# A gated delta rule on TensorE: products of 128 rows issued together, then products of 64 rows with the two heads by turns

## The chip, the cores and the metric

One core of a Trainium2 chip runs the whole program in one launch. The metric is the device time of that core in microseconds, the median of the runs shown.

## What is computed

The kernel is two layers of a block for a latent diffusion model, on 256 context tokens and 256 latent tokens of 1024 channels, in float32. Each layer has an input projection, four token mixers that read it (retention, HGRN2, the gated delta rule, RG-LRU), a merge with gates and an output projection, and then a feed-forward part with a convolution. The change touches the gated delta rule only. It has 4 heads with keys of 64 and values of 128 channels, scanned forward and backward, in chunks. One chunk of one head and direction, cut to what matters:

```python
def step(s, inp):
    qc, kc, vc, gc, bc = inp
    cum = jnp.cumsum(gc, axis=-1)
    rel = cum[..., :, None] - cum[..., None, :]
    a_mat = eye + (bc[..., :, None] * jnp.exp(jnp.where(strict, rel, -jnp.inf))
                   * jnp.einsum('bhtd,bhsd->bhts', kc, kc))
    rhs = bc[..., None] * (vc - jnp.exp(cum)[..., None] * jnp.einsum('bhtd,bhde->bhte', kc, s))
    u = lax.linalg.triangular_solve(a_mat, rhs, left_side=True, lower=True, unit_diagonal=True)
    qk = jnp.einsum('bhtd,bhsd->bhts', qc, kc) * jnp.exp(jnp.where(incl, rel, -jnp.inf))
    o = (jnp.exp(cum)[..., None] * jnp.einsum('bhtd,bhde->bhte', qc, s)
         + jnp.einsum('bhts,bhse->bhte', qk, u))
    last = cum[..., -1:]
    s_new = (jnp.exp(last)[..., None] * s
             + jnp.einsum('bhsd,bhse->bhde', kc * jnp.exp(last - cum)[..., None], u))
    return s_new, o
```

## The kernel before

The program writes its own order: jobs of large matrix products (projections, feed-forward; tiles gft, gtf, up) and threads of steps (the mixers, the layernorms) are emitted one step at a time by a loop that keeps an estimate of the engines' clocks and gives TensorE large products wherever a thread's step could not start yet (pump, L244). The order is fixed when the program is built; on the chip every engine works through its own queue in order and waits on semaphores. Nearly all instructions are issued through one helper, so the profile gives them line L82 and they are told apart by their tiles.

The delta rule (gdn, L1786) handles two heads at a time (group g, heads hh = 0 and 1), with a kernel chunk of 128 tokens. Per layer there are two groups, each with two segments (context, then latents) of two chunks. After the triangular systems are inverted (tile gd_T) the function recur (L2001) does one step of both directions d:

- U, a PSUM bank per head: for each direction a product of 128 rows, gd_T with the values (tile gd_v; L2012), and, when there is a state S already, a product of 64 rows, gd_W with gd_S (L2014). Head 0's operands of 64 rows lie in partitions 0 to 63, head 1's in 64 to 127. VectorE multiplies each head's bank by beta into gd_u (L2016).
- gd_dS (L2023), products with 64 columns per head, and from it the new state gd_S on VectorE (L2030) or, in the first step of a scan, ScalarE.

After both steps of a segment the readout (L2056 to L2067) forms gd_o, again a bank per head: for each chunk and direction a product of 128 rows (gd_P with gd_u) and, where that step had a state, one of 64 rows (gd_QT with gd_S). The function readout (L1272) then takes the squares (ro_sq, ScalarE, one instruction per head), the sums and the root on VectorE, scales (ro_n) and transposes on TensorE (ro_t). The last layer has no readout for the context.

The product call on float32 operands turns into two weight loads and two matmul records in the trace, so "x2" in a row is one product of the program. Products that only use 64 rows are marked 64\*128 there, those with 64 weight columns 128\*64, full ones 128\*128. A similar pair of heads exists elsewhere: gd_pk (L1884), the products of keys and queries, is issued head 0 first, then head 1, 64 rows each, one bank per head.

The loop that orders the two kinds of product in U is:

```python
for hh in range(2):
    U = self.pmt([128, 2, 128], "gd_U")
    for d in range(2):
        mm(U[:, d, :], R["TT"][...], v[...], start=True, stop=(S is None))
        if S is not None:
            mm(U[:, d, :], R["W"][p0:p0 + 64, ...], S[p0:p0 + 64, d, :], start=False, stop=True)
    V.tensor_tensor(u[:, :, hh, :], U, bb, op=ALU.mult)
```

PSUM banks for these come from one pool of four that all mixers share (pmt, L463).

Of the kernel before, what the change touches and what calls it, by code (L numbers as in the profile page):

```python
# [9 lines left out]
F32 = mybir.dt.float32  # L10
# [4 lines left out]
ALU = mybir.AluOpType  # L15
# [35 lines left out]
# by layer: the instances that follow one another in a pool  # L51
# [4 lines left out]
# the second layer's modulation blocks that fill the layernorms' waits  # L56
# [5 lines left out]
# from an engine's end to the start of the one that waits for it  # L62
# [9 lines left out]
class _Eng:  # L72
    """An engine of nc; every call also goes to the order's estimate of the engines' clocks."""
# [30 lines left out]
class _Pair:  # L104
    """the context's and the latents' jobs of one block"""
# [9 lines left out]
class Net:  # L115
# [17 lines left out]
    # ------------------------------------------- estimate of the engines' clocks  # L133
    def after(self, table, name, key):
        """when an engine sees that a tile is written (rdy) or read (rd)"""
        return max([t + LAT[p][key] for p, t in table.get(name, {}).items()] + [0.0])

    def names(self, x):
        """what the estimate knows an operand by: its tile, and the blocks of 256 for the activations"""
        nm = x.tensor.name  # L140
        if nm not in self.by_seg:
            return [nm]
        us = [x.offset // 256]
        for st, c in x.ap[1:-1]:
            us = [u + st // 256 * q for u in us for q in range(c)]
        st, n = x.ap[-1]
        m = (x.offset % 256 + st * (n - 1)) // 256 + 1
        return [f"{nm}.{u + q}" for u in us for q in range(m)]

    def account(self, key, name, a, k):  # L150
# [12 lines left out]
        if not dma:  # L163
            # engines take turns at a PSUM tile
# [72 lines left out]
    # ------------------------------------------------------------- the order  # L237
# [6 lines left out]
    def pump(self, until):  # L244
        """Emit the threads' steps and, where the tensor engine would wait for them, steps of matrix products."""
        while not until():
            # the step that can start first; products of matrices when none can start before the tensor engine is free
# [12 lines left out]
    def advance(self, t):  # L260
        outer, self.now_in = self.now_in, t
        try:
            t[1] = next(t[0])
            # a step's third word: the thread's bank is not used any more
# [6 lines left out]
    def finish(self, t, bank=False):  # L271
        """emit the rest of a thread, or its steps up to the last use of its bank"""
# [4 lines left out]
    def limit(self, key, n):  # L277
        """at most n threads of a kind are under way"""
# [5 lines left out]
    def when(self, t):  # L284
        """the engine of a thread's next step and the time when its operands are there (None: it waits for other steps)"""
# [8 lines left out]
    # -------------------------------------------------- matrix products' stream  # L294
# [20 lines left out]
    def feed(self):  # L315
        """keep loads three tiles ahead and splits two tiles ahead of the tile in use"""
# [15 lines left out]
    def splitter(self):  # L332
        """thread: the loaded tiles' two float32r parts, one tile ahead of the tile in use"""
# [15 lines left out]
    def gemm_start(self):  # L349
        """when the next step of the matrix products can start (None: it waits for a thread's step)"""  # L350
# [35 lines left out]
    def drain(self, jobs):  # L386
        """emit until these jobs are done"""
        self.pump(lambda: all(j.done for j in jobs))

    def store(self, pairs, then=None):  # L390
        """a thread that sends tiles to DRAM, [(to, from)], when they are there, so that the queue does not wait for them"""
# [25 lines left out]
    def evac(self, rec, ps, f, eng="ACT"):  # L417
        """a thread that empties a bank of products; its job is done when the thread is"""
# [13 lines left out]
    # --------------------------------------------------------------- helpers  # L432
# [5 lines left out]
    def xw(self, i, q, sg, d, n):  # L438
        """part q of blocks d .. d + n of a segment's modulated activations, to be written"""
        if i == 0:  # L440
            return self.X[0][q][:, d:d + n, sg * 256:(sg + 1) * 256]
        if sg not in self.X[i]:
            # a tile per segment: the context's place is used again
# [3 lines left out]
    def xr(self, q, k, t0, t1):  # L447
        """part q of block k of tokens t0 .. t1, as [(operand, first column)]"""
# [17 lines left out]
    def pgt(self, shape, name):  # L466
        """a bank of products and the list that its thread goes into"""
# [8 lines left out]
    def e2(self, shape, name, dt=F32):  # L476
        """a tile that lives within one step"""
        return self.tile(self.ep, shape, dt, "e2", name, 2)

    def ev(self, shape, name):  # L480
        """an evacuation thread's tile"""
# [23 lines left out]
    def load_consts(self):  # L505
        const, I, V, A, S = self.const, self.I, self.V, self.A, self.S
        # silu(c): columns (lat, ctx) and zeros up to a column tile of the tensor engine
# [25 lines left out]
    def derive(self):  # L533
        """small per-layer parameters"""
        const, V, A = self.const, self.V, self.A
        self.pd = []
        for i in range(DEPTH):
# [15 lines left out]
            hg = const.tile([128, 2, 8], F32, name=f"hgp{i}")   # B, -B with 1 - f = B - B tanh, B = (1 - lb) / 2  # L553
# [25 lines left out]
    def softplus(self, x, shape):  # L579
        """max(x, 0) + log1p(exp(-|x|)), log1p(e) = ln(w) + (e - (w - 1)) / w with w = 1 + e"""  # L580
# [17 lines left out]
    def rsq(self, v, n, scale=1.0, eps=EPS, post=None):  # L598
        """(v * scale + eps) ** -0.5 by a seed from the exponent bits and two Newton steps, the first one's constants fitted to the seed"""
# [18 lines left out]
    def tt(self, out, a, b, op, bias=POOL_BIAS):  # L618
        """tensor_tensor on the vector engine or on GpSimd, the one that would be done first"""
# [8 lines left out]
    def split(self, dstH, dstL, src32):  # L628
        """src32 into two float32r parts"""
# [3 lines left out]
    # ------------------------------------------------------- matrix products  # L633
    def gemm_ft(self, ps, HL, xH, xL, K, w=128, c0=0):
        """ps[f, t] = sum_k w[k, f] x[k, t], the weights stationary"""
# [3 lines left out]
        for k in range(K):  # L639
            h = H[:, k * w + c0:k * w + c0 + 128]  # L640
            for p, x in enumerate(xH(k) + xL(k)):
                # a start clears the written bits of the whole bank
# [13 lines left out]
    def in_ft(self, i, c0, tsl, evac, cond=None):  # L656
        """job: the [f, t] block of the input projection's columns c0 .. c0 + 128"""
# [11 lines left out]
    def gemm_tf(self, nks, tl, lH, lL, evac, eng="DVE"):  # L669
        """[t, 256 columns], the activations stationary, the weights moving; a bank holds two t tiles"""  # L670
# [4 lines left out]
        for n, nk in enumerate(nks):  # L675
            H, L = self.next_tile()
            for t in tl:
# [5 lines left out]
                for k in range(nk):  # L683
                    w = H[:, k * 256:(k + 1) * 256]
                    # a start clears the written bits of the whole bank
# [18 lines left out]
    # ------------------------------------------------------------- modulation  # L704
    def mod_jobs(self, i, nb, early=False):
        """512 columns nb of silu(c) @ w_mod[i]: shift and scale columns, or the gates' rows (kept in DRAM)"""
# [3 lines left out]
        def mk(kk):  # L710
            def run():
# [11 lines left out]
                # four rows' blocks side by side in the column tiles  # L723
# [8 lines left out]
            def evac(ps):  # L732
# [3 lines left out]
                if kind in (2, 5):  # L736
# [7 lines left out]
                    # half the gates: the products that they take carry the sigmoids' factor 2  # L744
# [20 lines left out]
    # -------------------------------------------------------------- layernorm  # L765
    def ln_rs(self, st):
        """(mean, 1 / std) of each token tile, from st [128, tile, groups, 6]"""
# [7 lines left out]
    def modulate(self, i, half, sg, xs):  # L775
        """layernorm0(x) * (1 + scale) + shift of segment sg, transposed to [d, t], in two float32r parts"""
# [48 lines left out]
    def seen(self, i, half, t0, t1):  # L825
        """whether the modulated activations of tokens t0 .. t1 are there"""
        return lambda: all((i, half, sg) in self.ok for sg in range(t0 // 256, (t1 + 255) // 256))

    def residual(self, i, half, xin, segs, when=lambda: True):
        """what the residual's sum needs beside the sub-layer's output"""  # L830
        self.grow = {}

        def load():
            yield when
            n = self.n_ran
            for sg in segs:
                if xin is not None:
                    self.r[sg] = self.tile(self.fa, [128, 2, 1024], F32, "f_r", "r", len(segs))
                    for j in range(2):
                        # a piece per job, between the weights  # L840
# [5 lines left out]
                # segment 0 is the context, column 1 of the modulation pair  # L846
# [37 lines left out]
    # ------------------------------------------------------------------ layers  # L884
    def body(self):
# [3 lines left out]
        # the first blocks' shift and scale go first  # L889
# [30 lines left out]
    def masks(self):  # L920
        """the masks, as bytes"""
# [8 lines left out]
    def mixers(self, prev):  # L930
# [24 lines left out]
        def closer():  # L955
            """the previous phase's end; then the space is there for the second group of mixers"""
# [50 lines left out]
    def merge_jobs(self, j, nm, pool):  # L1007
        """merged += sigmoid(gate) * (branch @ w_branch); the final branch also splits the sums"""
# [1214 lines left out]
```

## Time and profile before

| | before |
|---|---|
| median of 3 runs | 2274.57 us (2270.27 to 2276.27) |
| profiled execution, span from first to last instruction | 2267.0 us |
| median less that span (what lies around the span; no other time of the profiled execution is recorded) | 7.6 us |
| TensorE matmul busy | 2085.0 us, 92% of the span |
| VectorE, ScalarE, GpSimd busy | 1503.0, 870.1, 717.8 us |
| mean granted TensorE clock | 0.964 of full speed |

TensorE (PE) is the busiest engine; its weight loads (PEld) overlap its matmuls. In a timeline row the first number is the start in us from the start of the span, the second the time from the first start to the last end of the merged instructions. A matmul's recorded duration includes its way through the pipeline, so the pace of the engine is read from starts, not from durations.

### The profile page before, as it was taken

To read this page: it belongs to the slowest core of one execution; us is meant where nothing else is said; L and a number is where in the kernel's file an instruction comes from. 1 tells how busy PE (TensorE), PEld (TensorE's weight loads), DVE (VectorE), ACT (ScalarE), POOL (GpSimd) and SP (SyncE) were. 2 spreads that over 40 slices of the span, in tenths; PEclk is the share of its full clock that TensorE was granted. 3 is DMA by queue.
4 is the path that set the end of the run, shared out by engine and by line. 5 is a ranking of instruction groups with operands and counts; after the bars stand their busy time and mean duration, and the time that the engine had idled before them with its cause. 6 is when DMAs were issued, how large, how long until landed. Compare 5 with 4: busy or idle time off the path is not lost.

```text
span 2267.0 us, 35537 instructions
## 1 busy us (share of the span) xinstructions
PE 2085.0 (92%) x14052; PEld 1819.1 (80%) x14052; DVE 1503.0 (66%) x2380; ACT 870.1 (38%) x1277; POOL 717.8 (32%) x606
## 2 busy tenths in 40 slices
PE   6999899999999989879999986998998999888997
PEld 4767677877898968768898885887888889877997
DVE  6677346444383868976646688786375485878877
ACT  4555223222233233334423434664243323324553
POOL 1227422631130434420010032483247243513511
PEclk9999999999999999979999998999999999999999
DMA  7655325443314257554232344354234413566553
GB/s 296 202 171 161 126 64 161 120 148 103 120 64 136 83 174 248 160 176 128 91 98 93 98 154 159 111 161 139 83 120 129 135 33 98 177 234 209 180 187 118
DMA packets 133384, 320.14 MB, mean 141 GB/s; under 512 B 32961, under 2 KB 55265, under 8 KB 133217
## 3 DMA queue, kind: packets, MB, share of 16 engines
q1 hardware_dynamic: 119600, 289.76, 39.5%
q0 software_dynamic: 3712, 13.03, 1.8%
q10 hardware_dynamic: 9904, 15.08, 1.8%
q8 instruction: 111, 1.82, 0.3%
q14 instruction: 57, 0.46, 0.1%
HBM read 294.70 MB, written 23.10 MB: 140 GB/s over the span
## 4 chain that ended last, share of the span: by engine, by line
PE 64%; DVE 18%; POOL 5%; DMA 5%; issue 4%; ACT 3%; SPq 0%; ACTq 0%; DVEq 0%; POOLq 0%
PE gft L82 18%; PE gtf L82 15%; PE up L82 14%; PE mg_b L82 3%; DVE r L82 2%; POOL gd_x L82 2%; POOL gd_z L82 2%; DVE ffy L82 2%; DMA wraw<-in_wt 2%; PE hg_s L82 2%; DVE rq L82 2%; PE gd_U L82 2%; PE gd_o L82 2%; DMA br<-brd 1%; PE modp L82 1%
## 5 line engine op out<-in xcount | busy, mean ns | idle before, releaser
L82 POOL TENSOR_TENSOR wL<-wraw,wH 128x1024 fp32r<-128x1024 f32 (+2 forms) x143 | 335.7, 2351 | 890.3 <-ACT wH L82 756.5
L82 ACT ACTIVATE wH<-wraw 128x1024 fp32r<-128x1024 f32 (+2 forms) x395 | 408.0, 1036 | 216.2 <-PE gtf L82 130.5
L82 DVE TENSOR_TENSOR wL<-wraw,wH 128x1024 fp32r<-128x1024 f32 (+1 forms) x252 | 328.3, 1307 | 122.6 <-ACT wH L82 122.1
L82 PE MATMUL gft<-xmH,wH 128*128 128x512 f32 (+1 forms) x544 | 214.3, 398 | 3.8 <-ACT wH L82 3.8
L82 PE MATMUL gft<-xmL,wH 128*128 128x512 f32 (+1 forms) x544 | 205.5, 382 | 0.0
L82 PE MATMUL gft<-xms,wH 128*128 128x256 f32 x1344 | 188.3, 293 | 12.4 <-ACT lru_g L82 4.6
L82 PEld LDWEIGHTS gft<-xms,wH 128*128 128x128 f32 x1344 | 173.9, 198 | 18.1 <-ACT lru_g L82 4.8
L82 DVE SCALAR_TENSOR_TENSOR ffy<-up,parf,ffy 128x255 f32<-128x255 f32 (+1 forms) x188 | 110.9, 590 | 84.2 <-ACT ffy L82 79.5
L82 PE MATMUL up<-xmH,wH 128*128 128x512 f32 (+1 forms) x400 | 146.5, 373 | 13.6 <-DVE ffy L82 6.8
L82 PE MATMUL up<-xmL,wH 128*128 128x512 f32 (+1 forms) x400 | 146.1, 372 | 1.7 <-DVE xmL L82 1.7
L82 PEld LDWEIGHTS gft<-xmH,wH 128*128 128x128 f32 x544 | 103.7, 191 | 41.4 <-issue 16.7
L82 PE MATMUL gtf<-wH,hidH 128*128 128x256 f32 x528 | 132.0, 282 | 0.3 <-ACT wH L82 0.3
L82 PE MATMUL gtf<-wH,hidL 128*128 128x256 f32 x528 | 131.7, 282 | 0.0
L82 PE MATMUL gft<-xmH,wL 128*128 128x512 f32 (+1 forms) x544 | 131.3, 383 | 0.2 <-POOL wL L82 0.2
L82 PE MATMUL gtf<-wH,xmH 128*128 128x256 f32 x448 | 117.6, 294 | 9.6 <-DVE gy L82 9.0
L82 PEld LDWEIGHTS gft<-xmL,wH 128*128 128x128 f32 x544 | 103.8, 191 | 17.8 <-issue 0.7
L82 PEld LDWEIGHTS gft<-xmH,wL 128*128 128x128 f32 x544 | 98.2, 190 | 19.9 <-issue 1.3
L82 PE MATMUL gtf<-wH,xmL 128*128 128x256 f32 x448 | 113.6, 285 | 0.0
L82 ACT ACTIVATE ffy<-up,parf 128x256 f32<-128x256 f32 (+1 forms) x94 | 61.0, 648 | 120.2 <-PE up L82 120.0
L82 PE MATMUL mg_b<-brH,wH 128*128 128x256 f32 (+1 forms) x288 | 92.1, 338 | 13.4 <-ACT brH L82 9.1
L82 PEld LDWEIGHTS gtf<-wH,hidH 128*128 128x128 f32 x528 | 100.0, 189 | 0.6 <-ACT wH L82 0.5
L82 PEld LDWEIGHTS up<-xmH,wH 128*128 128x128 f32 x400 | 78.7, 197 | 26.7 <-issue 12.8
(335 smaller groups left out, 4677.9 us busy)
## 6 DMA issues: line engine op xcount, KB each, us to landing
wraw<-in_wt SPq DMA_DIRECT2D x467, 512.0 KB, 3.8
thd<-mg_t ACTq DMA_DIRECT2D x32, 256.0 KB, 2.2
mg_th<-thd SPq DMA_DIRECT2D x32, 256.0 KB, 4.1
wraw<-in_wt SPq DMA_DIRECT2D x20, 384.0 KB, 3.0
lnw<-in_rows POOLq DMA_DIRECT2D x8, 512.0 KB, 6.3
thd<-mg_t ACTq DMA_DIRECT2D x32, 128.0 KB, 2.6
xmm<-thd SPq DMA_DIRECT2D x16, 256.0 KB, 6.5
brd<-ro_b SPq DMA_DIRECT2D x28, 128.0 KB, 1.9
```

The lines of the kernel that those rows point to most:

```text
L82: r = f(*a, **k)
```

## The change

In recur both heads' banks are taken first, the four products of 128 rows are issued, then the four of 64 rows, direction by direction with the heads by turns, and then the two multiplications on VectorE. In the readout the eight products of 128 rows come first, head by head, then those of 64 rows with the heads by turns. The start and stop marks of the accumulation move accordingly: one start per bank.

```diff
-            for hh in range(2):
-                p0 = 64 * hh
-                U = self.pmt([128, 2, 128], "gd_U")
-                for d in range(2):
-                    c = 2 * seg + cs[d]
-                    mm(U[:, d, :], R["TT"][:, 2 * cs[d] + hh, 1 - d, :], v[:, c, hh * 128:(hh + 1) * 128], start=True, stop=(S is None))
-                    if S is not None:
-                        mm(U[:, d, :], R["W"][p0:p0 + 64, cs[d], d, :], S[p0:p0 + 64, d, :], start=False, stop=True)
+            U = [self.pmt([128, 2, 128], "gd_U") for _ in range(2)]
+            for hh in range(2):
+                for d in range(2):
+                    mm(U[hh][:, d, :], R["TT"][:, 2 * cs[d] + hh, 1 - d, :], v[:, 2 * seg + cs[d], hh * 128:(hh + 1) * 128],
+                       start=(d == 0), stop=(S is None and d == 1))
+            if S is not None:
+                for d in range(2):
+                    for hh in range(2):
+                        p0 = 64 * hh
+                        mm(U[hh][:, d, :], R["W"][p0:p0 + 64, cs[d], d, :], S[p0:p0 + 64, d, :], start=False, stop=(d == 1))
+            for hh in range(2):
                 bb = _cap(be, (2 * seg + cs[0]) * 8 + 2 * g + hh, [[(cs[1] - cs[0]) * 8 + 4, 2], [0, 128]])
-                V.tensor_tensor(u[:, :, hh, :], U, bb, op=ALU.mult)
+                V.tensor_tensor(u[:, :, hh, :], U[hh], bb, op=ALU.mult)
...
-                po = []
+                po = [(self.pmt([128, 2, 128], "gd_o"), slice(hh, 4, 2)) for hh in range(2)]
+                step = lambda cc, d: cc if d == 0 else 1 - cc
+                late = [(cc, d, hh) for cc in range(2) for d in range(2) for hh in range(2) if Ss[step(cc, d)] is not None]
                 for hh in range(2):
-                    p0 = 64 * hh
-                    po.append((self.pmt([128, 2, 128], "gd_o"), slice(hh, 4, 2)))
-                    for cc in range(2):
-                        ops = []
-                        for d in range(2):
-                            n = cc if d == 0 else 1 - cc
-                            ops.append((P[d][:, 2 * cc + hh, :], us[n][:, d, hh, :]))
-                            if Ss[n] is not None:
-                                ops.append((R["QT"][p0:p0 + 64, cc, d, :], Ss[n][p0:p0 + 64, d, :]))
-                        for k, (a, b) in enumerate(ops):
-                            mm(po[hh][0][:, cc, :], a, b, start=(k == 0), stop=(k == len(ops) - 1))
+                    for cc in range(2):
+                        for d in range(2):
+                            mm(po[hh][0][:, cc, :], P[d][:, 2 * cc + hh, :], us[step(cc, d)][:, d, hh, :], start=(cc == 0 and d == 0),
+                               stop=(cc == 1 and d == 1 and not late))
+                for k, (cc, d, hh) in enumerate(late):
+                    p0 = 64 * hh
+                    mm(po[hh][0][:, cc, :], R["QT"][p0:p0 + 64, cc, d, :], Ss[step(cc, d)][p0:p0 + 64, d, :], start=False,
+                       stop=not any(x[2] == hh for x in late[k + 1:]))
```

What moves is seen on TensorE's queue. The first place is the second step of the first scan (layer 0, first two heads, context): gd_U_2578 is head 0's bank, gd_U_2579 (2584 before) head 1's.

```order
-L82 MATMUL gd_U_2578<-gd_v_1075,gd_T_1264 128x128
+L82 MATMUL gd_U_2578<-gd_v_1075,gd_T_1264 128x128 x2
+L82 MATMUL gd_U_2579<-gd_v_1075,gd_T_1264 128x128 x2
 L82 MATMUL gd_U_2578<-gd_S_2555,gd_W_2506 128x128
-L82 MATMUL gd_U_2578<-gd_v_1075,gd_T_1264 128x128
+L82 MATMUL gd_U_2579<-gd_S_2555,gd_W_2506 128x128
 L82 MATMUL gd_U_2578<-gd_S_2555,gd_W_2506 128x128
-L82 MATMUL gd_U_2584<-gd_v_1075,gd_T_1264 128x128
-L82 MATMUL gd_U_2584<-gd_S_2555,gd_W_2506 128x128
-L82 MATMUL gd_U_2584<-gd_v_1075,gd_T_1264 128x128
-L82 MATMUL gd_U_2584<-gd_S_2555,gd_W_2506 128x128
+L82 MATMUL gd_U_2579<-gd_S_2555,gd_W_2506 128x128
```

The eight products stay between the same neighbours; the two kinds no longer alternate, and the second kind alternates between the heads' banks.

The second place is the readout right behind it, still on TensorE; gd_o_2615 is head 0's bank, gd_o_2616 (2622 before) head 1's.

```order
+L82 MATMUL gd_o_2615<-gd_u_2577,gd_P_2611 128x128
+L82 MATMUL gd_o_2615<-gd_u_2523,gd_P_2613 128x128
+L82 MATMUL gd_o_2616<-gd_u_2523,gd_P_2611 128x128
+L82 MATMUL gd_o_2616<-gd_u_2577,gd_P_2613 128x128
+L82 MATMUL gd_o_2616<-gd_u_2577,gd_P_2611 128x128
+L82 MATMUL gd_o_2616<-gd_u_2523,gd_P_2613 128x128
 L82 MATMUL gd_o_2615<-gd_S_2555,gd_QT_2513 128x128
-L82 MATMUL gd_o_2615<-gd_u_2577,gd_P_2611 128x128
+L82 MATMUL gd_o_2616<-gd_S_2555,gd_QT_2513 128x128
 L82 MATMUL gd_o_2615<-gd_S_2555,gd_QT_2513 128x128
```

The twelve products of this readout are the same twelve; the four with gd_QT now come last, by turns. On VectorE, ScalarE, GpSimd and SyncE no instruction changes its place in its queue.

## Rows read from the trace of the kernel before

**Rows 1.** The page: busy time by engine, and the chain that ended last.
```profile
PE 2085.0 (92%) x14052; PEld 1819.1 (80%) x14052; DVE 1503.0 (66%) x2380; ACT 870.1 (38%) x1277; POOL 717.8 (32%) x606
...
PE 64%; DVE 18%; POOL 5%; DMA 5%; issue 4%; ACT 3%; SPq 0%; ACTq 0%; DVEq 0%; POOLq 0%
```

**Rows 2.** Busy time by stretch: from:to, length, then us per engine, clock, DMA.
```profile
260.00:560.00 300.00, 295.25 (x1893) 234.44 (x1892) 144.63 (x325) 82.07 (x130) 106.54 (x119) 0.99 0.37 114
1560.00:1860.00 300.00, 281.28 (x2133) 259.48 (x2131) 176.41 (x312) 100.88 (x164) 118.02 (x119) 0.97 0.34 106
```

**Rows 3.** Timeline of PE: a step's U with a state (start, us, what).
```profile
272.52 0.39 PE L82 MATMUL gd_U<-gd_v,gd_T 128*128 128x128 f32 x2
272.83 0.48 PE L82 MATMUL gd_U<-gd_S,gd_W 64*128 64x128 f32 x2
273.25 0.49 PE L82 MATMUL gd_U<-gd_v,gd_T 128*128 128x128 f32 x2
...
275.33 0.48 PE L82 MATMUL gd_U<-gd_S,gd_W 64*128 64x128 f32 x2
275.75 0.39 PE L82 MATMUL gtf<-wH,xmH 128*128 128x256 f32 x1
```

**Rows 4.** Timeline of PE: a readout with four products of 64 rows.
```profile
277.37 0.66 PE L82 MATMUL gd_dS<-gd_u,gd_kt 128*64 128x128 f32 x8
277.96 0.71 PE L82 MATMUL gd_o<-gd_u,gd_P 128*128 128x128 f32 x4
278.60 0.49 PE L82 MATMUL gd_o<-gd_S,gd_QT 64*128 64x128 f32 x2
...
282.21 0.36 PE L82 MATMUL gtf<-wH,xmH 128*128 128x256 f32 x1
```

**Rows 5.** Timeline of PE: a readout with eight products of 64 rows, first and last.
```profile
320.62 0.39 PE L82 MATMUL gd_o<-gd_u,gd_P 128*128 128x128 f32 x2
...
326.77 0.48 PE L82 MATMUL gd_o<-gd_S,gd_QT 64*128 64x128 f32 x2
327.19 0.39 PE L82 MATMUL gtf<-wH,xmH 128*128 128x256 f32 x1
```

**Rows 6.** All matmuls of these tiles and the multiplication behind them: ns min/median/max.
```profile
L82 PE MATMUL gd_U<-gd_S,gd_W x96: 272/373/579, 272.8 to 1844.1; 64*128 64x128 f32 x96
L82 DVE TENSOR_TENSOR gd_u<-gd_U,gd_be x32: 392/425/426, 268.2 to 1845.4; 128x256 f32<-128x256 f32 x32
L82 PE MATMUL gd_o<-gd_u,gd_P x96: 270/275/377, 278.0 to 1852.6; 128*128 128x128 f32 x96
L82 PE MATMUL gd_o<-gd_S,gd_QT x80: 272/322/373, 278.6 to 1853.1; 64*128 64x128 f32 x80
```

**Rows 7.** Timeline of PE: a step without a state, layer 1.
```profile
1804.25 1.05 PE L82 MATMUL gd_U<-gd_v,gd_T 128*128 128x128 f32 x8
1805.06 1.19 PE L82 MATMUL gft<-xms,wL 128*128 128x256 f32 x8
1806.18 0.55 PE L82 MATMUL gd_dS<-gd_u,gd_kt 128*64 128x128 f32 x6
```

**Rows 8.** Timeline of PE: gd_pk, four products of 64 rows, two per head.
```profile
1453.96 0.72 PE L82 MATMUL gd_pk<-gd_kq 64*128 64x128 f32 x8
1454.61 1.55 PE L82 MATMUL lru_gp<-lru_x,lru_w 128*128 128x512 f32 x3
```

**Rows 9.** Timeline of DVE: the multiplications of the step in rows 7.
```profile
1804.89 0.87 DVE L82 TENSOR_TENSOR gd_u<-gd_U,gd_be 128x256 f32<-128x256 f32 x2 [1.45 <-PE gd_U L82]
```

**Rows 10.** Timeline of ACT: the squares of the readout in rows 4.
```profile
280.38 0.38 ACT L82 ACTIVATE ro_sq<-gd_o 128x256 f32<-128x256 f32 x1 [9.02 <-PE gd_o L82]
282.49 0.39 ACT L82 ACTIVATE ro_sq<-gd_o 128x256 f32<-128x256 f32 x1 [1.73 <-PE gd_o L82]
```

**Rows 11.** What PE waited for, whole span: us in total, times, longest.
```profile
PE ro_t L82 <- DVE ro_n L82: 10.0, 7, 4.0
PE gd_dS L82 <- DVE gd_u L82: 1.9, 1, 1.9
```

**Rows 12.** DVE's idle time before gd_u (us, times).
```profile
  PE gd_U L82: 47.6, 24
```

**Rows 13.** The core's span and clock, and a stretch with a lower clock.
```profile
core 0: 2267.0 us, clock 0.964
...
1758.00:1790.00 32.00, 28.67 (x207) 28.47 (x207) 14.94 (x25) 11.59 (x19) 8.18 (x16) 0.85 0.61 198
```

## The prediction

> **What bounds the kernel.** I read the page first, for the engine that matters: TensorE is busy 92% of the span and makes up 64% of the chain that ended last, VectorE 18% [rows 1]. An average can mislead, so the next view is busy time by stretch. The delta rule's steps lie in 260 to 560 us and 1560 to 1860 us, and there TensorE is busy 295.25 and 281.28 of 300 us while VectorE has 144.63 and 176.41 [rows 2]. The large products that fill TensorE's queue have no gaps between them, so TensorE time that goes away here moves everything behind it forward, unless a wait opens. Then the timeline of TensorE, for what one step costs.
>
> The reader should look at starts. In a step with a state, the products of 128 and of 64 rows alternate, two records each, and every group starts 0.42 us after the one before: 272.83, 273.25, and so on to 275.75 [rows 3]. Where eight records of 128 rows follow one another, the next work starts after 0.81 us, so 0.10 us per record, or 0.20 per pair [rows 7]. The alternation therefore costs about 0.2 us at each turn: the engine does not start a 64-row product before the 128-row ones have left it, nor the other way round. The whole step takes 275.75 - 272.52 = 3.23 us [rows 3]. A readout with four products of 64 rows takes 282.21 - 277.96 = 4.25 us [rows 4], one with eight 327.19 - 320.62 = 6.57 us [rows 5]. How often: 96 records of the state's product are 12 steps of 8 [rows 6]; 96 of the P products are 6 readouts of 16, and 80 of the QT products fill two readouts with 8 and four with 16 [rows 6].
>
> **The change, part by part.** Nothing is added or removed; no engine but TensorE gets another order. Its cost is the new length of the 18 blocks.
>
> The part of 64 rows has its own row. gd_pk is the same shape and count: four products of 64 rows, two per head in the two halves of the array, a bank per head. Eight records take 1454.61 - 1453.96 = 0.65 us to the start of the next work, the leaving included [rows 8]. Eight in single file at 0.10 to 0.11 us would need 0.8 to 0.9 plus the 0.2 of the turn, so the heads' records run side by side there, about 0.11 us per pair.
>
> - Step with a state: the first pair of 128 rows up to the first 64-row start is 0.31 us [rows 3]; six more records at 0.11 make 0.97; the 64-row part is 0.65. Sum 1.62 us against 3.23, a gain of 1.61, 12 times: 19.3 us.
> - Readout with four products of 64 rows: four P records with entry and leaving take 278.60 - 277.96 = 0.64 us [rows 4]; twelve more at 0.11 make 1.96; with 0.65 it is 2.61 against 4.25. Gain 1.64, twice: 3.3 us.
> - Readout with eight: 0.31 + 14 x 0.11 = 1.85 for the P records; 0.65 + 4 pairs x 0.11 = 1.09 for the others. Sum 2.94 against 6.57. Gain 3.63, four times: 14.5 us.
>
> Together 37.1 us of TensorE. The pace is a choice: 0.10 of rows 7 for all of them would add 1.5 us (72 + 24 + 56 records counted above), which is the upper bound, 38.6. I take 0.11 because the gaps in rows 3 fit it: 0.42 less the 0.2 of the turn, over two.
>
> A rule of the Trainium skill bears on the 64-row part (TensorE: Matmul & The Clock Gate, Part 3: Packing small matmuls): matmuls start and end strictly in program order. By it, with two records per product, head 1's first record could only start with head 0's second, and eight records would need five slots and not four: 18 blocks times 0.11 is 2.0 us less gain, 35.1. By that rule gd_pk, which issues all of head 0 first, would hardly overlap at all; rows 8 show that it does, so the sum stays.
>
> What is given back. Before, head 0's bank was multiplied by beta on VectorE while TensorE still worked on head 1; now both banks are finished at the end. The step without a state already is in that order: its two multiplications take 0.87 us and end at 1805.76 [rows 9], 0.70 us after the block's end at 1805.06, and TensorE needs them at 1806.18, with 0.42 us to spare [rows 7]. A step with a state ends in the same way, with large products of 1.1 to 1.6 us behind it, so this is hidden, except where VectorE is late: one such wait of 1.9 us exists before [rows 11]. I take 0.7 us for all of them. Bounds: nothing, and 0.70 x 12 = 8.4 us if nothing covered them.
>
> In the readout the squares of head 0 ran beside head 1's products (280.38, against 282.49 for head 1 [rows 10]); now both come at the end and the chain to ro_t gets 0.38 us longer. TensorE already waits for ro_n seven times, 10.0 us [rows 11], so this counts: 6 x 0.38 = 2.3 us, between nothing and that. Both heads' banks are now needed at the start of a block, from the pool of four; at worst TensorE waits earlier for the same release as before, which takes part of a block's gain and can't make it longer than it was. I cost it at nothing, covered by products between the last reader and the block. The other way, VectorE sat idle 47.6 us for gd_U in front of what was queued behind gd_u [rows 12]; that falls by about half, which can only help, and I count nothing for it.
>
> Sum: 37.1 - 0.7 - 2.3 = 34.1 us off a span of 2267.0, so 2232.9; the runs' median lies 7.6 us above that span, and 2274.6 - 34.1 = 2240.5 us.
>
> **The rivals.**
> 1. *The work behind becomes late.* VectorE and ScalarE get both heads at once, and TensorE arrives earlier at everything that does not depend on it (substitution on GpSimd, DMA landings). If nothing covers the multiplications, 8.4 + 2.3 = 10.7 us go, and 26.4 remain: 2248. For it: the 1.9 us wait [rows 11]. Against it: TensorE's 4.75 us of idle in 300 [rows 2], and rows 7. The Trainium skill (TensorEngine Tiling (Array Packing), Performance Considerations, PSUM Bottleneck) says that packing speeds up TensorE and not the emptying of PSUM, which may then bound; by that rule this rival is the outcome, 2248; the rows give it less weight, since the multiplications end 0.42 us before they are needed.
> 2. *The heads do not overlap when they also add to a bank that 128-row products began.* In single file at 0.11, each block of eight 64-row records is 0.44 longer (0.88 less 0.44), each of sixteen 0.88: 14 x 0.44 + 4 x 0.88 = 9.7 us less, gain after the give-back 24.4: 2250. If each turn of heads also costs 0.2 us, a product of 64 rows costs 0.42 and the parts 1.7 and 3.3 us in place of 0.65 and 1.09: 14 x 1.05 + 4 x 2.2 = 23.5 less: 2264. That would be the change not doing what its words say. Against both: rows 8.
> 3. *More than the sum*, by freed VectorE and ScalarE that shorten other waits: 40 us or more, 2235 and below. For it: rows 12. Against: hardly any idle time on TensorE to win there [rows 2].
> 4. *Slower, by the clock.* TensorE's granted clock is 0.964 over the span and 0.85 in 1758 to 1790 us, where it works 28.67 of 32 us [rows 13]: of the two levels, 1.2 and 2.4 GHz, the lower one held 0.15 x 2 x 32 = 9.6 us there, at up to 4.8 us of lost work. If TensorE, arriving early, waits longer at such places and its clock falls, time is lost with no wait to show. To turn a gain of 34 into a loss of 7 it takes 41 us, some nine more such stretches, a mean clock below 0.964 - 41/2267 = 0.946; the time is then 2281 or more. Against: the blocks themselves get denser, and the clock was 0.99 in 260 to 560 [rows 2].
>
> **How the numbers follow.** Forecast (2236 to 2246): 0.62. Rival 1: 0.17. Rival 2: 0.08. Rival 3: 0.08. Absorbed altogether, within 0.3% (6.8 us, about what a measurement of this kernel can tell from no change): 0.02. Rival 4: 0.03. The predicted time is the likeliest case's, 2240.5. The range goes down to 2231 (the full 38.6 and a few us of rival 3; the runs before alone spread over 6 us) and up to 2254, which takes in rival 1 and the first half of rival 2. Faster by over 0.3% in all but the last two cases: 0.95; same 0.02; slower 0.03.
>
> **What would show it right or wrong.** In the changed profile a step with a state should read as eight gd_v records, then eight gd_S records as one row, about 1.6 us to the next work, with the state's records paired at nearly one start; the readouts 2.6 and 2.9 us. If the eight 64-row records take about 1.1 us they went in single file (rival 2), at 1.7 each turn drains. Waits of gd_dS for gd_u, or of ro_t for ro_n, above 12 us in all would be rival 1; a mean clock under 0.955 points to rival 4. If the blocks are as short as said and the time falls by much less than 30 us, my step "TensorE time here moves the end" is the one that failed.

## The result and the profile after

| | before | after |
|---|---|---|
| median, runs of the first comparison | 2272.42 us (4 runs) | 2236.86 us (4 runs, 2232.16 to 2238.51) |
| ratio, 95% interval | | 0.9849 [0.9824, 0.9873] |
| span of the profiled execution | 2267.0 us | 2230.3 us |
| TensorE matmul busy | 2085.0 us | 2045.1 us |
| mean granted TensorE clock | 0.964 | 0.966 |

The change takes 35.6 us off the median and 36.7 us off the span. The forecast was 2240.5 us, in a range of 2231 to 2254. The profiled execution of the changed kernel took 2232.16 us for a span of 2230.3, so only 1.9 us lie around a span. The 7.6 us that the prediction put there were for the most part the difference between the profiled execution of before and the median of its runs.

The page after, the same lines as in [rows 1]:

```profile
PE 2045.1 (92%) x14052; PEld 1796.9 (81%) x14052; DVE 1505.2 (67%) x2380; ACT 869.0 (39%) x1277; POOL 716.1 (32%) x606
...
PE 62%; DVE 20%; POOL 5%; DMA 4%; issue 4%; ACT 4%; SPq 0%; ACTq 0%; DVEq 0%; POOLq 0%
```

TensorE lost 39.9 us of busy time; its share stays 92% because the span shrank with it. The other engines did the same work. The busy time by stretch, for the windows that hold the delta rule (the second one earlier by what was gained before it), against [rows 2]:

```profile
260.00:560.00 300.00, 294.76 (x1977) 239.64 (x1976) 147.11 (x328) 88.81 (x139) 105.02 (x117) 0.99 0.41 127
1530.00:1830.00 300.00, 278.10 (x2250) 263.56 (x2249) 187.60 (x330) 106.89 (x174) 120.36 (x123) 0.98 0.35 109
```

TensorE is as full as before and has done more in the same time: 1977 and 2250 matmul records where 1893 and 2133 fitted. TensorE's timeline, the same step and readout as in [rows 3] and [rows 4], and the readout of [rows 5]:

```profile
271.05 1.05 PE L82 MATMUL gd_U<-gd_v,gd_T 128*128 128x128 f32 x8
272.03 0.72 PE L82 MATMUL gd_U<-gd_S,gd_W 64*128 64x128 f32 x8
272.68 0.39 PE L82 MATMUL gtf<-wH,xmH 128*128 128x256 f32 x1
...
274.89 2.05 PE L82 MATMUL gd_o<-gd_u,gd_P 128*128 128x128 f32 x16
276.87 0.71 PE L82 MATMUL gd_o<-gd_S,gd_QT 64*128 64x128 f32 x8
277.52 0.39 PE L82 MATMUL gtf<-wH,xmH 128*128 128x256 f32 x1
...
312.82 1.95 PE L82 MATMUL gd_o<-gd_u,gd_P 128*128 128x128 f32 x16
314.70 1.16 PE L82 MATMUL gd_o<-gd_S,gd_QT 64*128 64x128 f32 x16
315.79 0.39 PE L82 MATMUL gtf<-wH,xmH 128*128 128x256 f32 x1
```

Read the starts. The step takes 272.68 - 271.05 = 1.63 us where it took 3.23, and eight 64-row records take 272.68 - 272.03 = 0.65 us, exactly what gd_pk took in [rows 8]. The readouts take 2.63 and 2.97 us where they took 4.25 and 6.57.

The waits of TensorE that the prediction named, against [rows 11], and one that it did not:

```profile
PE ro_t L82 <- DVE ro_n L82: 10.0, 7, 4.0
...
PE hg_s L82 <- DVE hg_k L82: 3.9, 6, 1.1
...
PE gd_dS L82 <- DVE gd_u L82: 1.9, 1, 1.9
```

The two waits of the prediction are the same in sum. The third, for hg_k, was 2.0 us in four waits before; the two new ones come from the last delta-rule group of the second layer, here on TensorE's timeline:

```profile
1807.89 1.06 PE L82 MATMUL gd_U<-gd_v,gd_T 128*128 128x128 f32 x8
1808.88 0.71 PE L82 MATMUL gd_U<-gd_S,gd_W 64*128 64x128 f32 x8
1810.49 1.13 PE L82 MATMUL hg_s<-hg_Q,hg_k 128*128 128x128 f32 x8 [0.89 <-DVE hg_k L82]
...
1812.88 0.38 PE L82 MATMUL gd_o<-gd_u,gd_P 128*128 128x128 f32 x2
1813.79 1.83 PE L82 MATMUL gd_o<-gd_u,gd_P 128*128 128x128 f32 x14 [0.52 <-DVE gd_P L82]
1815.55 1.16 PE L82 MATMUL gd_o<-gd_S,gd_QT 64*128 64x128 f32 x16
1817.80 0.46 PE L82 MATMUL hg_s<-hg_Q,hg_k 128*128 128x128 f32 x2 [1.09 <-DVE hg_k L82]
```

and what VectorE did meanwhile:

```profile
1809.13 2.88 DVE L82 TENSOR_TENSOR hg_k<-hg_k,hg_G 128x512 f32<-128x512 f32 x2
1811.94 0.74 DVE L82 TENSOR_TENSOR gd_u<-gd_U,gd_be 128x256 f32<-128x256 f32 x2
1812.60 1.13 DVE L82 TENSOR_TENSOR gd_P<-gd_A,ck 128x512 f32<-128x512 f32 x1
```

Here the HGRN2 mixer keeps VectorE busy: gd_u starts 4.05 us after U began and 2.35 us after its last product ended. TensorE does not wait for gd_u itself but for hg_k and gd_P, which stand around it in VectorE's queue (0.89, 0.52 and 1.09 us in the rows). This step takes 2.59 us to the next work, and the readout behind it 4.91, so 0.96 and 1.94 us of the gain are lost to these waits and the restarts behind them. In all other blocks the gain is whole.

### The profile page after: what moved, and what is told of

The parts are those of the page before. It is cut to its first block, busy times and chain, and to the rows that moved or that the text cites. A ratio compares the mean times of both kernels' runs of the same rounds, so it can differ in the third digit from the quotient of the medians.

```text
span 2230.3 us, 35537 instructions
## 1 busy us (share of the span) xinstructions
PE 2045.1 (92%) x14052; PEld 1796.9 (81%) x14052; DVE 1505.2 (67%) x2380; ACT 869.0 (39%) x1277; POOL 716.1 (32%) x606
## 4 chain that ended last, share of the span: by engine, by line
PE 62%; DVE 20%; POOL 5%; DMA 4%; issue 4%; ACT 4%; SPq 0%; ACTq 0%; DVEq 0%; POOLq 0%
PE gft L82 17%; PE gtf L82 14%; PE up L82 14%; PE mg_b L82 4%; DVE r L82 2%; POOL gd_z L82 2%; POOL gd_x L82 2%; DVE ffy L82 2%; DVE rq L82 2%; PE hg_s L82 2%; DMA br<-brd 1%; PE modp L82 1%; ACT wH L82 1%; DVE hg_k L82 1%; DMA thd<-mg_t 1%
```

## The experiments

Each of these kernels was timed in five rounds against the kernel before on the same chip. The first four shared one set of runs of before, the last three another.

| run | median, us | before, us | ratio, 95% interval | profiled span, us |
|---|---|---|---|---|
| steps alone | 2249.46 | 2274.05 | 0.9895 [0.9875, 0.9916] | 2248.8 |
| readouts alone | 2255.82 | 2274.05 | 0.9921 [0.9898, 0.9944] | 2247.5 |
| grouped, no turns of heads | 2235.56 | 2274.05 | 0.9838 [0.9816, 0.9860] | 2235.0 |
| one half of the array | 2242.54 | 2274.05 | 0.9869 [0.9848, 0.9890] | 2241.4 |
| kinds alternate, heads by turns | 2244.41 | 2273.24 | 0.9877 [0.9859, 0.9896] | 2241.7 |
| the changed kernel again | 2232.88 | 2273.24 | 0.9824 [0.9803, 0.9845] | 2231.3 |
| retention in pairs too | 2231.12 | 2273.24 | 0.9820 [0.9795, 0.9845] | 2229.4 |

The intervals are some 8 to 11 us wide, about as wide as the differences between several variants. So the blocks' lengths in the traces carry the finer argument and the times the coarse one.

**Steps alone, readouts alone.** In the first the readouts keep the loop of before, in the second the steps do:

```diff
 # steps alone: the readout as before
...
-                for k, (cc, d, hh) in enumerate(late):
...
+                        for k, (a, b) in enumerate(ops):
+                            mm(po[hh][0][:, cc, :], a, b, start=(k == 0), stop=(k == len(ops) - 1))
...
 # readouts alone: the step as before
-            U = [self.pmt([128, 2, 128], "gd_U") for _ in range(2)]
...
             for hh in range(2):
...
+                U = self.pmt([128, 2, 128], "gd_U")
...
```

> Only the steps (gd_U) are in the new order, the readouts as before. Theory (each turn between 128-row and 64-row products costs about 0.2 us, the heads' 64-row products run side by side, and TensorE time here moves the end): 12 steps with a state at 1.63 in place of 3.23 us, 18 to 19 us less than before, about 2254 beside a before of 2272.4. Rival (the two multiplications by beta, now both behind the block, are waited for): up to 8.4 us of that is given back, about 2262, with waits of gd_dS for gd_u.

> Only the readouts (gd_o) are in the new order, the steps as before. Theory: 2.63 and 2.97 us in place of 4.25 and 6.57, 17.6 us less on TensorE, about 2255 to 2257, so that this and the run with the steps alone add up to the whole gain of some 35 us. Rival (the squares of both heads now behind the block make the transposes late): 2.3 us less gain, about 2259, with more waits of ro_t for ro_n than 10.0 us.

Measured: 24.6 and 18.2 us less than before by the medians, 18.2 and 19.5 us by the profiled spans. Outside the last group, the steps are 1.63 us long in the first and the readouts 2.63 and 2.97 in the second; the part left alone kept its old length in each. The waits are 1.9 us for gd_u in the first and 10.0 us for ro_n in the second, as before. Both rivals, about 2262 and 2259, lack the waits that they needed. The time excludes the first as well (2246 to 2255 by its interval); the second time alone, 2251 to 2261, would not have told. The spans' gains add to 37.7 against 36.7 for both together, so as far as the profiles tell the two parts add up. The 24.6 us of the medians is above the 18 to 19 that were expected of the steps. The profiled spans, at granted clocks of 0.966 and 0.964, agree with the expectation; over all executions the median clock was 0.962 before and 0.9655 with the steps alone, and what that is worth is read below, at the changed kernel's second comparison.

**Grouped, but without turns of the heads.**

```diff
-                for d in range(2):
-                    for hh in range(2):
+                for hh in range(2):
+                    for d in range(2):
                         p0 = 64 * hh
...
-                late = [(cc, d, hh) for cc in range(2) for d in range(2) for hh in range(2) if Ss[step(cc, d)] is not None]
+                late = [(cc, d, hh) for hh in range(2) for cc in range(2) for d in range(2) if Ss[step(cc, d)] is not None]
```

> Both blocks are grouped by kind, but the 64-row products go head 0 first, then head 1. Theory (the two halves of the array take their products side by side even when all of one head's are queued ahead, as in gd_pk): no change from the changed kernel, 2237 within 2 us, and eight 64-row records still take 0.65 us. Rival (matmuls start strictly in program order, so that only the last record of head 0 meets the first of head 1): eight take about 0.33 us more, sixteen 0.77 more, 14 x 0.33 + 4 x 0.77 = 7.7 us, about 2245.

Measured: 38.5 us less than before, as much as with turns. The steps still take 1.64 us, with head 0's four records queued ahead of head 1's four, but the large readouts take 3.52 us and not 2.97. TensorE's timeline of one step and one large readout of this kernel:

```profile
272.14 0.72 PE L82 MATMUL gd_U<-gd_S,gd_W 64*128 64x128 f32 x8
272.80 0.39 PE L82 MATMUL gtf<-wH,xmH 128*128 128x256 f32 x1
...
314.84 1.71 PE L82 MATMUL gd_o<-gd_S,gd_QT 64*128 64x128 f32 x16
316.48 0.39 PE L82 MATMUL gtf<-wH,xmH 128*128 128x256 f32 x1
```

The step's eight records take 0.66 us, so head 1's products start beside head 0's although they stand behind them. The readout's sixteen take 1.64 us where turns take 1.09. The single starts, which the merged row hides, show why: the first start of the other half comes 0.55 us after the first of all, together with the fifth of head 0's eight. TensorE looks ahead, but not over eight records; between four and eight nothing was tried. Neither theory is whole: the strict order is refuted by the step, and "queued ahead is as good" by the large readout. Turns are worth 0.55 us in three of the four large readouts, 1.6 us in all, and nothing elsewhere, which is below what the times can tell. The fourth, in the last group, takes 4.90 us here and 4.91 with turns, since it waits for VectorE in both.

**Both heads in one half of the array.** Head 1's 64-row products read head 0's rows; what head 1's state adds to U and gd_o is replaced by head 0's.

```diff
                     for hh in range(2):
-                        p0 = 64 * hh
+                        p0 = 0
                         mm(U[hh][:, d, :], R["W"][p0:p0 + 64, cs[d], d, :], S[p0:p0 + 64, d, :], start=False, stop=(d == 1))
...
-                    p0 = 64 * hh
+                    p0 = 0
                     mm(po[hh][0][:, cc, :], R["QT"][p0:p0 + 64, cc, d, :], Ss[step(cc, d)][p0:p0 + 64, d, :], start=False,
```

> As the changed kernel, but head 1's 64-row products read head 0's rows (partitions 0 to 63), so that both heads use the same half of the array; head 1's state does not enter its sums. Theory (the halves working side by side are worth 0.44 us per eight records): 14 x 0.44 + 4 x 0.88 = 9.7 us more than the changed kernel, about 2246.5, eight 64-row records at 1.1 us. Rival (only the turns between the kinds of product matter): 2237 and 0.65 us.

Measured: 2242.54 us, 7.0 us more than the kernel without turns beside it, 31.5 less than before. TensorE's timeline:

```profile
273.66 1.05 PE L82 MATMUL gd_U<-gd_v,gd_T 128*128 128x128 f32 x8
274.65 1.16 PE L82 MATMUL gd_U<-gd_S,gd_W 64*128 64x128 f32 x8
275.73 0.39 PE L82 MATMUL gtf<-wH,xmH 128*128 128x256 f32 x1
...
318.86 2.05 PE L82 MATMUL gd_o<-gd_S,gd_QT 64*128 64x128 f32 x16
320.84 0.39 PE L82 MATMUL gtf<-wH,xmH 128*128 128x256 f32 x1
```

Eight records in single file take 275.73 - 274.65 = 1.08 us and sixteen 1.98, 0.43 and 0.89 more than in two halves. So working side by side is 14 x 0.43 + 4 x 0.89 = 9.6 us of the gain on TensorE, and grouping by kind the rest, about three quarters of the whole. The last group, which waits for VectorE anyway, absorbs a part of it: its step took 2.59 us and its readout 4.90 here too. The 18 blocks of this trace are 6.8 us longer in sum than those of the kernel without turns, and the time rose by 7.0.

**Kinds alternate, heads by turns.**

```diff
-            for hh in range(2):
-                for d in range(2):
...
+            for d in range(2):
+                for hh in range(2):
                     mm(U[hh][:, d, :], R["TT"][:, 2 * cs[d] + hh, 1 - d, :], v[:, 2 * seg + cs[d], hh * 128:(hh + 1) * 128],
                        start=(d == 0), stop=(S is None and d == 1))
-            if S is not None:
-                for d in range(2):
+                if S is not None:
                     for hh in range(2):
                         p0 = 64 * hh
...
```

The products of 128 rows go direction by direction here, too, and the readout is changed in the same way.

> The heads by turns as in the changed kernel, but the products of 128 and 64 rows alternate direction by direction: four turns of kind in a step in place of two, eight in a readout with eight 64-row products. Theory (the price is per turn of kind): a step 0.53 + 0.43 + 0.64 + 0.43 = 2.0 us, the large readout 4.15, the small one 3.1; 12 x 0.39 + 4 x 1.18 + 2 x 0.47 = 10.3 us more than the changed kernel, about 2247. Rival (the heads by turns alone bring the gain): 2237.

Measured: 2244.41 us, 11.5 more than the changed kernel beside it (10.3 expected). A step takes 2.02 us, a large readout 4.15 and a small one 3.04, against 2.0, 4.15 and 3.1 expected. TensorE's timeline of a step:

```profile
271.75 0.61 PE L82 MATMUL gd_U<-gd_v,gd_T 128*128 128x128 f32 x4
272.29 0.49 PE L82 MATMUL gd_U<-gd_S,gd_W 64*128 64x128 f32 x4
272.71 0.71 PE L82 MATMUL gd_U<-gd_v,gd_T 128*128 128x128 f32 x4
273.35 0.49 PE L82 MATMUL gd_U<-gd_S,gd_W 64*128 64x128 f32 x4
273.77 0.39 PE L82 MATMUL gtf<-wH,xmH 128*128 128x256 f32 x1
```

The same sixteen records with two more turns of kind cost 2.02 - 1.63 = 0.39 us more, 0.2 per turn. The large readouts have eight turns in place of two and cost in proportion: six more, 1.18 us. The price is per turn, and turns of heads within one kind cost nothing.

**The changed kernel again.**

> The changed kernel itself once more, beside the others on the same chip: 34 to 36 us less than before, about 2237. If the clock had given part of the first comparison's gain, this one would be some us smaller.

Measured: 40.4 us less, by the interval 35.2 to 44.8, against the 34 to 36 expected. The blocks have the same lengths as in the first trace, but for one step of the second layer that ran in part at the lower clock: 2.51 us at a granted clock of 0.62, where the first trace has 1.97 at 0.82. The clock over the span was 0.967. The gain is not one lucky comparison.

Its size by the times needs the clock beside it. The 20 recorded executions of the kernel before in these two sets reach from a span of 2262.7 us at a clock of 0.966 to one of 2277.2 at 0.957; a straight line through all 59 executions of the table and the first comparison, fitted within each kernel, gives 1.3 us per 0.001 (an estimate). In this comparison the median clock was 0.960 before and 0.966 after, so some 8 of the 40.4 us go with the clock, and of the 24.6 us of the steps alone some 4.5. Executions at the same clock compare better: at 0.966 one of before took 2262.7 us and three of the changed kernel 2227.7, 2230.3 and 2230.8; at 0.964 it is 2266.0 and 2268.4 against 2232.8 and 2236.2. At the four clocks that both have, the change takes 31 to 34 us off, which is what the blocks gave. The sign named in the expectation, a smaller gain, could not show this, because here the kernel before had the lower clock.

**Retention in pairs too.** An attempt at a version that beats both: the scores of retention are 64-row products as well, and went one head after the other.

```diff
-            for sb in range(4):
-                yield [q, k] + tab
...
-                ps = self.pmt([128, 512], "ret_s")
-                mm(ps[:, :n], k[p0:p0 + 64, sb * 128:(sb + 1) * 128], q[p0:p0 + 64, t0:512], start=True, stop=True)
...
+        for sb in range(4):
+            yield [q, k] + tabs[0] + tabs[1]
...
+            pss = [self.pmt([128, 512], "ret_s") for _ in range(2)]
+            for hh in range(2):
+                p0 = 64 * hh
+                mm(pss[hh][:, :n], k[p0:p0 + 64, sb * 128:(sb + 1) * 128], q[p0:p0 + 64, t0:512], start=True, stop=True)
...
```

> The changed kernel, and in the retention mixer the scores (ret_s, 64 rows) of both heads issued as pairs, so that they run side by side too; the order of everything around is planned anew. Theory (64-row products in two halves at the same time are worth half their TensorE time wherever they stand): ret_s goes from about 18.8 us (4 x 2.77 and 4 x 1.92) to about 10, so 8 to 9 us less than the changed kernel, about 2228. Rival (the new plan and the later start of head 1's readout cost as much as is saved): 2237 or more.

Measured: 2231.12 us beside 2232.88, no difference. Here VectorE sets the pace. One pair of heads in this kernel, TensorE, then two of its weight loads, then VectorE:

```profile
415.57 4.71 PE L82 MATMUL ret_s<-ret_r 64*128 64x512 f32 x16
420.22 0.64 PE L82 MATMUL modp<-wraw,cz 128*32 128x256 f32 x8
```

```profile
418.27 0.29 PEld L82 LDWEIGHTS ret_s<-ret_r 64*128 64x128 f32 x2 [0.37 <-issue]
418.93 0.30 PEld L82 LDWEIGHTS ret_s<-ret_r 64*128 64x128 f32 x2 [0.36 <-issue]
```

```profile
416.74 4.06 DVE L82 TENSOR_TENSOR ret_P<-ret_s,ret_tab 128x256 f32<-128x256 f32 x12 [8.72 <-PE ret_s L82]
```

Two heads take 420.22 - 415.57 = 4.65 us, where one head alone takes 2.77 in the changed kernel, so 0.9 us is gained where half of 5.5 was hoped for. Twelve multiplications of VectorE empty the banks in one unbroken run of 4.06 us, while TensorE has only the mixers' pool of four banks to run ahead in: its first four products run side by side, the last four start one at a time, 0.66 us apart, about what two multiplications take that empty a bank (4.06 / 12 x 2 = 0.68). No run had a larger pool. All retention scores together take 16.0 us and not 19.2 (the sum over their blocks, start to next work), and the program planned anew keeps none of the 3.2 us that a measurement could tell. There is no version here that is clearly better than the changed kernel.

## Why the prediction was right

**The bound.** "TensorE time that goes away here moves everything behind it forward" held. From the start of a block to the next work, the sum over the 16 steps fell from 42.8 to 24.4 us and over the 6 readouts from 34.7 to 19.1: 34.1 us in all, the waits inside included, against 36.7 on the span and 31 to 34 at equal clock.

**The terms.** 1.61, 1.64 and 3.63 us per block were forecast, and 1.60, 1.62 and 3.60 measured. Taking the length of the 64-row part whole from a row of the same shape, gd_pk, instead of building it from records, kept this close: the eight records take 0.65 us in both. Both halves of the reason now stand on their own experiments: 0.2 us per turn of kind (kinds alternate), and side by side against single file (one half of the array). Rival 2 is thereby out. The turns of heads matter in the large readouts only.

**The rule on program order.** The sentence of the Trainium skill (TensorE: Matmul & The Clock Gate, Part 3: Packing small matmuls) that matmuls start strictly in program order did not hold in the run without turns: there a 64-row product of the second half starts beside one that stands four records ahead of it. The prediction's choice of the row over the rule was right, and the measurement gives the rule's remainder: the look-ahead ends before eight records.

**What is given back.** The total, 3.0 us forecast against 2.9, came out right by luck: neither of its two terms came as priced, and the loss that did come was priced at nothing.

The squares first. "The squares of head 0 ran beside head 1's products ... so this counts: 2.3 us" was too large. ScalarE now does the two in one go, in the readout of [rows 4]:

```profile
277.62 0.66 ACT L82 ACTIVATE ro_sq<-gd_o 128x256 f32<-128x256 f32 x2 [7.74 <-PE gd_o L82]
```

They end 0.76 us after the block's end at 277.52, where head 1's square alone ended 282.49 + 0.39 - 282.21 = 0.67 after it [rows 4] [rows 10]; in the large readouts it is 0.76 against 0.49. So the chain grew by 0.09 and 0.27 us, not by 0.38. Also, only four of the seven waits for ro_n stand behind readouts of the delta rule: 1.04, 0.87, 1.50 and 0.85 us before, 1.10, 1.13, 1.69 and 0.27 after. Three grew by 0.5 us together, and the fourth, in the last group, shrank by 0.6, so the sum of 10.0 hides both.

The 0.7 us for late multiplications was priced as waits of gd_dS for gd_u, and these stayed at 1.9 us. The 2.9 us were lost where TensorE now comes early to other work that needs VectorE, hg_s and the products with gd_P in the last group of the second layer; the prediction has that only in the general sentence of rival 1, without a price. Rows of the kernel before could have told it. There, too, VectorE is still in HGRN2's multiplications when this block ends, TensorE first and then VectorE:

```profile
1843.85 0.48 PE L82 MATMUL gd_U<-gd_S,gd_W 64*128 64x128 f32 x2
```

```profile
1842.27 2.89 DVE L82 TENSOR_TENSOR hg_k<-hg_k,hg_G 128x512 f32<-128x512 f32 x2
1845.08 0.74 DVE L82 TENSOR_TENSOR gd_u<-gd_U,gd_be 128x256 f32<-128x256 f32 x2
```

A look at what VectorE did around each of the 18 blocks, and not at one typical block, would have shown it. That VectorE's idle time in front of gd_u would fall by half was too much, too: 47.6 us [rows 12] became 35.1.

**The rivals.** The prices of rival 1 (8.4 + 2.3 us) were not paid: the waits that it named are 11.9 us in all, as before. Its general sentence, that TensorE arrives earlier at everything that does not depend on it, came true in one group of four. The sentence of the Trainium skill on emptying PSUM (TensorEngine Tiling (Array Packing), PSUM Bottleneck) does not describe the delta rule's blocks, but it describes the retention run, where VectorE's 4.06 us bound a pair of heads. Rival 4 did not happen: the clock was 0.966. Rival 3 did not happen as it was meant, by shorter waits: TensorE's waits over the whole span went from 167.5 to 171.0 us (all rows added), 2.5 of the 3.5 us more are the new ones in the last group, and the others did not become shorter in sum. What the span lost beyond the blocks lies in TensorE's other products: the same instructions, their waits taken out, took 2007.2 us before and 2003.9 after, and 113.5 and 104.7 us of that were at the lower of the two clock levels. A mean clock of 0.966 in place of 0.964 is worth 0.036 x 2267 - 0.034 x 2230 = 5.8 us of full-speed work, rounding apart, which is enough for these 3 us. Whether the change itself raised the clock stays open: the mean was 0.962 over the 20 executions of before and 0.965 over the eight of the changed kernel, but executions of the same kernel differ by more, and no run here set the clock.

## What to carry to other kernels

Products that use the whole array and products that use half of it should be issued in blocks of a kind: every change of kind cost 0.2 us here, about as much as a product of 128 columns itself (two records of 0.11 us). Within the half-array block, alternate the halves when more than four records would stand in a row on one side (four did no harm here, eight did), and check which engine empties the banks before hoping for the factor of two. To price such a block, look for one of the same shape elsewhere in the trace and take its length from the start of its first instruction to the start of the next work.

## What the runs showed of the hardware

- A turn between 128-row and 64-row products costs 0.2 us (0.39 us for two more turns in a step), in either direction: the groups of two records in [rows 3] start 0.42 us apart whichever kind follows; changing from one half of the array to the other within 64-row products costs nothing measurable.
- TensorE starts half-array products out of program order: with four records of one half queued ahead both halves start together (0.66 us for eight), with eight queued ahead the other half starts 0.55 us late (1.64 us for sixteen, 1.09 with turns).
- Executions of one program differ in the granted clock, and their spans go with it: 2277.2 us at 0.957 and 2262.7 at 0.966 for the kernel before. Gains of a per cent are best read at equal clock or from the lengths of the blocks.
- The time around the span of an execution is 1.7 to 1.9 us here; a median of runs should be compared with a profiled span only through the time of that same execution.
